# Dilated attention: input laid out by residues, and projections with the weights stationary

## The chip, the cores and the metric

The kernel runs on one core of a Trainium2 chip. The metric is the device time of one execution in microseconds (us); less is better. The core's engines are TensorE (PE, with its weight loads listed apart as PEld), VectorE (DVE), ScalarE (ACT), GpSimd (POOL) and SyncE (SP, which issues most of the transfers). [...]

## The reference

Two transformer blocks, one after the other, on 512 tokens of width 1024. The change lies in the first half of the second block, dilated attention:

```python
DILATED_PATTERNS = ((128, 1), (512, 4), (2048, 16))     # window, dilation
proj = (x @ w_in).reshape(B, S, 3 groups, 3 (q, k, v), 16 heads, 64)
for g, (window, dilation) in enumerate(DILATED_PATTERNS):
    q = rotary(proj[:, :, g, 0], pos)
    k = rotary(proj[:, :, g, 1], pos)
    o, lse = dilated_window_attention(q, k, proj[:, :, g, 2], window, dilation)
...
wts = softmax(stack(lses)); o = sum(wts * outs); return o @ w_out
```

In a group with dilation d a query sees itself and the 128 tokens before it that have the same residue modulo d (as far as they exist). `rotary` turns each head's two halves of 32 features against each other by an angle that depends on the token: `x1*cos - x2*sin` and `x2*cos + x1*sin`.

## The kernel before

Products in full precision are made of three matmuls (`mm3`, lines 161 to 163): every operand is kept as a high part and a low part, and high x high, high x low and low x high are summed in PSUM. Weights arrive by DMA in chunks of 1 MB (1024 rows, 256 columns), two buffers deep; ACT makes the high part (line 187) and DVE, now and then POOL, the low part (line 188), again two buffers deep.

The input of dilated attention, `xT`, is feature-major: tiles with features on the partitions and the 512 tokens as columns in their order. `turn` (line 417) fills it from the residual, one tile of 128 tokens at a time: transposes on PE (line 422), then the split into high (ACT, line 247) and low (DVE, line 248). Each is put off under a key until a step needs it.

`dilated` (line 1386) works in four rounds of four heads, that is two pairs of heads. In a round `project` makes nine chunks, queries, keys and values (s = 0, 1, 2) of three groups g, each with 256 columns of weights. A chunk is four steps, one for each tile of 128 tokens: `project_one` holds the tokens of `xT` stationary and moves 256 columns of weights past them, 8 feature blocks x 3 matmuls = 24 per step, 96 per chunk. For the values of the second and third group a step takes not a tile of neighbouring tokens but the tokens of one residue modulo 4: every fourth column of `xT` (`kx` with step 4).

The result of a step is token-major. Queries and keys are rotated there by DVE (four operations, lines 1436, 1438 and 1440), then turned to feature-major, as the scores want them: two transposes (line 1445), put off by two steps, and two copies by ACT (lines 1451 and 1457), which also sort the tokens by residue, except for the keys of the first group. Values stay token-major and are copied by ACT (lines 1425 and 1428).

33 steps of the first round run alone. After that the loop over rounds works through 16 units per round (a head and a block of 128 queries). `unit` emits, in this order: the scores of a unit (lines 1494 and 1501) with masked maximum, exponential and sum (lines 1482 to 1485); some projection steps of the next round (`fill(0)`); the transposes of the unit before it (`flip`, lines 1510 and 1512), with their copies out of PSUM by ACT (line 1514) and DVE (line 1515); more steps (`fill(1)`); the value products of that unit (lines 1526 and 1529). The fourth round's units are interleaved with the output projection instead. The order on each engine is fixed when the kernel is built, by a scheduler that follows the order of the code but can put an instruction whose operands are free earlier ahead of those that wait. Eight PSUM banks serve all of it.

Of the kernel before, what the change touches and what calls it, by code (L numbers as in the profile page):

```python
# [28 lines left out]
# ---------------------------------------------------------------- constants of the shapes  # L29
# [15 lines left out]
def constants():  # L45
# [11 lines left out]
    rot = np.concatenate([_tok_tiles(np.concatenate([c, c], 1)), _tok_tiles(np.concatenate([-s, s], 1))], 1)  # L57
# [22 lines left out]
    c4, i = rows // 32, rows % 32  # L80
    for j in range(4):
        t = 128 * j + 4 * i + c4
        first = 0 if j == 0 else 128 * (j - 1)
        keys = np.arange(first, 128 * (j + 1))
# [26 lines left out]
class Net:  # L111
# [14 lines left out]
    # ------------------------------------------------------------ small helpers  # L126
# [41 lines left out]
    def wchunk(self, segs, kt, n):  # L168
        """Weights [kt*128, n] gathered from column segments (part slice, k slice, column, source)."""
# [44 lines left out]
    def need(self, *keys):  # L214
        """Emits all that was put off up to the last of keys (all of it without keys)."""
# [3 lines left out]
    def only(self, key):  # L219
        """Emits what was put off under one key, ahead of the rest."""  # L220
# [15 lines left out]
    def rsqrt_act(self, st, scale, eps):  # L236
        """The same where the tables of ScalarE are not in use for exponentials."""
# [3 lines left out]
    def split_to(self, hi, lo, src):  # L241
        """src (SBUF, full precision) into its two parts."""
# [7 lines left out]
    # ------------------------------------------------------------ setup  # L250
    def setup(self):
# [34 lines left out]
        # the parts of a modulation's row stand two partitions apart  # L286
# [17 lines left out]
    def load_cols(self, names, eng):  # L304
        """Vectors of features as columns, turned from rows."""
# [39 lines left out]
    def mod_rows(self, ps, raw, more=False):  # L345
        """Four partial sums of the two rows of a modulation, 32 partitions apart."""
# [5 lines left out]
    def row_parts(self, out, ps):  # L352
        """Rows of a modulation, their high parts on partitions r of 32 and the low ones on r + 2."""
# [4 lines left out]
    def mod_unit(self, i, u):  # L358
        """Columns u*256.. of layer i's modulation: rows for a gate, else turned to per-feature columns."""
# [32 lines left out]
    def affine(self, i, which):  # L392
        """Per-feature factor and shift of the modulated norm, [128, 8, 2 (latent, context)]."""
# [21 lines left out]
    # ------------------------------------------------------------ norm and turn  # L415
    def turn(self, n, xh, xl, c0, a=None, b=None, every=2):
# [27 lines left out]
    def kx(x, k, c0, n, step=1):  # L444
        """k-th 128 features of pair tiles x = (hi, lo), columns c0.."""
        if step == 1:
            return x[0][k // 2][:, k % 2, c0:c0 + n], x[1][k // 2][:, k % 2, c0:c0 + n]
        return x[0][k // 2][:, k % 2, c0:c0 + (n - 1) * step + 1:step], x[1][k // 2][:, k % 2, c0:c0 + (n - 1) * step + 1:step]

    def ssq(self, x, hf, ss):  # L450
        """Sum of squares of half hf of x into ss[:, hf]."""
# [16 lines left out]
    # ------------------------------------------------------------ squared-relu MLP  # L468
    def mlp(self, width, xT, w1, w2, ranges, tiles, sink, lag=3):
# [16 lines left out]
        def chunk():  # L486
            """The next 256 hidden features: weights, and tiles of their parts."""
# [36 lines left out]
    def skew(tiles, lag):  # L524
        """(0, tile) and (1, tile) over the tiles, the second following the first by lag tiles."""
# [6 lines left out]
    # ============================================================ first block  # L532
# [3 lines left out]
    def gains(self, i):  # L536
        """Head gains on every partition."""
# [3 lines left out]
        n = 0  # L541
# [8 lines left out]
    def tables(self, at, eng):  # L550
        """Rope tables with the head gains folded in."""
# [23 lines left out]
    def rope(self, dst, ps, nh, tab, tt, tmp):  # L575
        """dst = gains and (for latent tokens, over the last rw columns) rotation of nh heads."""
# [16 lines left out]
    def heads(self, ps, nh, w, tab, tt, out, sq, t1, t2):  # L593
        """Normed, gained, rotated heads of ps [128, nh*w] into out [128, nh, w]."""
# [9 lines left out]
    # ------------------------------------------------------------ attention over all tokens  # L604
    def attention(self, i, jobs):
        """jobs: dicts of prep (emits what the job needs, returns (kind, q, k, v)), mix tile, fill steps."""
# [4 lines left out]
        def ring(tag, n, width, size):  # L611
            """Space n of a ring of size in the tiles of weights, which are taken as they are needed."""
# [68 lines left out]
        def emit(v, u):  # L681
            """Scores of unit v between the turns and products of unit u."""
# [35 lines left out]
    def mix_parts(self, j, m):  # L718
        """Half m of a pair of mixed features that was kept whole, into its parts."""
# [21 lines left out]
    def first(self, cols):  # L741
        """First layer: its input and the first projection, a quarter of the features at a time as their modulation
        comes in. Returns the input tiles and the projection's sums."""
# [47 lines left out]
        def units(s):  # L791
            """Rows of the modulation of quarter s."""
# [8 lines left out]
        def columns(s):  # L801
            """The modulation's columns of quarter s."""
# [19 lines left out]
        def features(s, tp):  # L822
            """The parts of the features of quarter s of a pair of token tiles."""
# [59 lines left out]
    def layer(self, i, xT, tab, sums=None):  # L883
# [32 lines left out]
        # ckv | kr | cq (first half)  # L916
# [20 lines left out]
        # cq (second half) | q heads 0 3  # L937
# [21 lines left out]
        # k heads | v heads  # L959
# [6 lines left out]
        # q heads 1 4 2 5  # L966
# [5 lines left out]
        def stacked(src, toks, hi, lo=None):  # L972
            """Pairs of heads turned into parts over both halves of the rows: hi with lo, or (hi, lo) each twice."""
# [16 lines left out]
        # pool input; meanwhile the keys of the heads that share them  # L990
# [28 lines left out]
        # second projections of the latent-rank heads, a pair of heads at a time  # L1019
# [97 lines left out]
        # output projection, gated into the residual  # L1117
# [8 lines left out]
        def weights(c):  # L1126
            """A quarter of the output projection's columns, rows as the mixed features lie."""
# [111 lines left out]
    # ============================================================ second block  # L1239
# [5 lines left out]
    def ln_rows(self, name, i):  # L1245
        """Gain and shift of a layer norm on every partition."""
# [13 lines left out]
    def ln_turn(self, j, name, i, rows, xT, wait=2, table=True):  # L1260
        """Layer norm of token tile j: to feature-major parts, and in place as the next residual."""
# [19 lines left out]
        def finish():  # L1281
            """The last norm of token tile j, out to memory."""
# [102 lines left out]
    # ------------------------------------------------------------ dilated attention  # L1385
    def dilated(self, xT):
# [6 lines left out]
        nc.sync.dma_start(m1[:, 512:1024], t["k_rot"])  # L1393
        rot = m1[:, 512:1024].rearrange("p (a t c) -> p a t c", a=2, t=4)
        masks = [m0[:, 0:192], m0[:, 192:576], m0[:, 576:1024], m1[:, 0:512]]

        def project(r, order):
            """Steps that project, rotate and turn the four heads of round r, two pairs; the tiles they fill."""
# [12 lines left out]
            def project_one(g, s):  # L1411
                c0 = (g * 3 + s) * 1024 + r * 256
                wc = self.wcols(w, [(c0, c0 + 256)])
                place(g, s)
                for j in range(4):
# [6 lines left out]
                    if s == 2:  # L1422
                        pv = ps.rearrange("p (a c) -> p a c", a=2)
                        if g == 2:
                            nc.scalar.activation(T["w"][:, :, j, :], pv, AF.Copy)
                        else:
# [461 lines left out]
```

## Time and profile before

| | before |
|---|---|
| median of 3 runs | 3301.78 us (3300.62 to 3303.79) |
| span of the profiled execution | 3301.2 us |
| time around that span | not listed by the profile |
| PE busy | 3238.5 us, 98% |
| PE weight loads | 2807.8 us, 85% |
| DVE busy | 1776.6 us, 54% |
| ACT busy | 1265.7 us, 38% |
| POOL busy | 376.2 us, 11% |
| moved by DMA | 281.62 MB, mean 85 GB/s |
| projections of dilated attention | about 1622 to 2240 us of the span |

All times come from one execution taken by the hardware profiler. Matmuls overlap: one starts while the one before it still drains, so PE's busy time says that PE was never empty, not how fast it went. How fast a stream goes is read from the distances between the starts of its matmuls.

### The profile page before, as it was taken

The page shows a single profiled execution, that of the slowest core. Times are in us where ns is not written, and L with a number is a line of the kernel's source. Part 1 is how long each engine was busy: PE and PEld are TensorE (multiplying, and loading weights), DVE is VectorE, ACT ScalarE, POOL GpSimd, SP SyncE. Part 2 cuts the span into 40 slices and gives each one's busy share as a digit, 9 for nine tenths or more (in the row PEclk, how much of TensorE's full clock was granted, in tenths as well). Part 3 has the DMA queues.
Part 4 walks back from the last instruction along what each step waited for, and adds up shares of the span by engine and source line. Part 5 has one row for each costly group of instructions (what it writes and reads, how often), then busy time and mean ns, then how long its engine had stood idle before and what let it go on. Part 6 is the DMA issues. An engine that isn't in the chain of part 4 may idle for free.

```text
span 3301.2 us, 52357 instructions
## 1 busy us (share of the span) xinstructions
PE 3238.5 (98%) x21704; PEld 2807.8 (85%) x21704; DVE 1776.6 (54%) x3550; ACT 1265.7 (38%) x2549; POOL 376.2 (11%) x541
## 2 busy tenths in 40 slices
PE   7999999999999999999999999999999999989998
PEld 6877988788889788888899999998888878888887
DVE  6677554444466866555644343435544467664445
ACT  4566432222236754222223333334322246542222
POOL 4343100000004420000000000001100030030000
PEclk9999999999999999999999999999999999999999
DMA  7132233333321022322321112112223222133332
GB/s 215 51 103 91 77 104 113 105 115 115 115 58 49 1 66 89 102 90 91 102 77 65 55 62 65 52 55 71 94 90 102 98 73 65 64 103 102 94 98 77
DMA packets 246509, 281.62 MB, mean 85 GB/s; under 512 B 19518, under 2 KB 208384, under 8 KB 246272
## 3 DMA queue, kind: packets, MB, share of 16 engines
q1 hardware_dynamic: 244528, 273.28, 26.0%
q10 hardware_dynamic: 1584, 4.98, 0.4%
q8 instruction: 171, 2.80, 0.4%
q14 instruction: 66, 0.54, 0.1%
q0 software_dynamic: 160, 0.02, 0.0%
HBM read 276.16 MB, written 2.10 MB: 84 GB/s over the span
## 4 chain that ended last, share of the span: by engine, by line
PE 80%; issue 11%; DVE 4%; ACT 2%; POOL 1%; DMA 1%; SPq 0%; ACTq 0%; DVEq 0%; POOLq 0%
PE b L161 18%; PE b L162 18%; PE b L163 18%; PE s L161 4%; PE s L163 4%; PE s L162 4%; PE b L671 2%; PE b L655 2%; PE b L349 1%; PE s L633 1%; DVE t L248 1%; DVE wl L188 1%; PE b L1529 1%; PE b L1445 1%; PE b L1526 1%
## 5 line engine op out<-in xcount | busy, mean ns | idle before, releaser
L161 PE MATMUL b<-wh,t 128*128 128x256 f32 (+2 forms) x2948 | 986.6, 335 | 1.5 <-ACT t L247 1.0
L162 PE MATMUL b<-wl,t 128*128 128x256 f32 (+2 forms) x2948 | 968.3, 328 | 3.9 <-DVE wl L188 3.9
L163 PE MATMUL b<-wh,t 128*128 128x256 f32 (+2 forms) x2948 | 968.8, 329 | 2.7 <-DVE t L248 2.7
L187 ACT ACTIVATE wh<-wr 128x2048 fp32r<-128x2048 f32 (+4 forms) x253 | 389.2, 1549 | 895.1 <-PE b L163 547.3
L188 DVE TENSOR_TENSOR wl<-wr,wh 128x2048 fp32r<-128x2048 f32 (+4 forms) x237 | 460.5, 1947 | 416.6 <-ACT wh L187 415.7
L161 PEld LDWEIGHTS b<-wh,t 128*128 128x128 f32 x2948 | 595.2, 202 | 53.8 <-issue 4.5
L162 PEld LDWEIGHTS b<-wl,t 128*128 128x128 f32 x2948 | 596.5, 202 | 44.3 <-DVE wl L188 4.5
L163 PEld LDWEIGHTS b<-wh,t 128*128 128x128 f32 x2948 | 595.9, 202 | 44.3 <-DVE t L248 3.5
L161 PE MATMUL b<-t,wh 128*128 128x512 f32 (+1 forms) x1232 | 440.8, 359 | 3.0 <-ACT t L247 3.0
L162 PE MATMUL b<-t,wh 128*128 128x512 f32 (+1 forms) x1232 | 439.4, 357 | 1.1 <-DVE t L248 1.1
L163 PE MATMUL b<-t,wl 128*128 128x512 f32 (+1 forms) x1232 | 439.1, 357 | 1.0 <-DVE wl L188 1.0
L161 PEld LDWEIGHTS b<-t,wh 128*128 128x128 f32 x1232 | 233.4, 190 | 39.7 <-ACT t L247 3.4
L163 PEld LDWEIGHTS b<-t,wl 128*128 128x128 f32 x1232 | 233.7, 190 | 35.6 <-DVE wl L188 1.4
L162 PEld LDWEIGHTS b<-t,wh 128*128 128x128 f32 x1232 | 233.7, 190 | 35.2 <-DVE t L248 1.6
L243 DVE CAST t<-h 128x512 fp32r<-128x512 f32 (+1 forms) x176 | 66.1, 377 | 241.2 <-ACT h L481 241.0
L480 ACT ACTIVATE h<-b 128x512 f32<-128x512 f32 (+1 forms) x138 | 70.8, 513 | 220.6 <-PE b L163 220.6
L1186 DVE TENSOR_TENSOR h<-b,gate 128x512 f32<-128x512 f32 (+1 forms) x141 | 89.0, 631 | 120.0 <-PE b L163 119.9
L161 PE MATMUL s<-wh,t 128*128 128x256 f32 (+2 forms) x428 | 146.8, 343 | 1.7 <-ACT h L927 1.0
L1321 DVE TENSOR_TENSOR xl<-xl,b 128x512 f32<-128x512 f32 x128 | 87.3, 683 | 111.3 <-PE b L163 111.3
L162 PE MATMUL s<-wl,t 128*128 128x256 f32 (+2 forms) x428 | 144.1, 337 | 0.0
L163 PE MATMUL s<-wh,t 128*128 128x256 f32 (+2 forms) x428 | 144.1, 337 | 0.0
L647 POOL TENSOR_SCALAR wl<-wl,st 128x768 f32<-128x768 f32 (+1 forms) x120 | 103.6, 864 | 160.6 <-DVE st L646 132.8
(363 smaller groups left out, 4515.5 us busy)
## 6 DMA issues: line engine op xcount, KB each, us to landing
wr<-in_w_mlp SPq DMA_DIRECT2D x64, 1024.0 KB, 5.3
wr<-in_w_mod SPq DMA_DIRECT2D x44, 1024.0 KB, 5.3
wr<-in_attn_w_in SPq DMA_DIRECT2D x36, 1024.0 KB, 5.0
wr<-in_ffn_w_up SPq DMA_DIRECT2D x32, 1024.0 KB, 5.4
wr<-in_ffn_w_down SPq DMA_DIRECT2D x32, 1024.0 KB, 5.0
wr<-in_hgrn_w_in SPq DMA_DIRECT2D x12, 1024.0 KB, 5.1
wr<-in_w_out SPq DMA_DIRECT2D x8, 640.0 KB, 5.1
wr<-in_w_in SPq DMA_DIRECT2D x4, 1024.0 KB
```

Of the source, the lines that this page charges most:

```text
L161: mm(out, a[0], b[0], start=start, stop=False)
L162: mm(out, a[0], b[1], start=False, stop=False)
L163: mm(out, a[1], b[0], start=False, stop=stop)
L187: nc.scalar.activation(hv, rv[:, k], AF.Copy)
L188: (self.aid if cut > 1 and m % 2 else nc.vector).tensor_sub(lv, rv[:, k], hv.bitcast(F32))
L243: self.nc.vector.tensor_copy(hi, src)
L480: nc.scalar.activation(r, ps, AF.Relu)
L647: nc.gpsimd.tensor_scalar(P[:, :n], P[:, :n], sm, 1.0, op0=ALU.mult, op1=ALU.mult)
L655: nc.tensor.transpose(ps[:, kk, a * 128:(a + 1) * 128], u["P"][e, a][:, k0:k0 + 128], self.ident)
L671: nc.tensor.matmul(u["O"][64 * e:64 * e + 64, :256], v[:, k, e * 64:(e + 1) * 64], u["PT"][e, k2][:, kk, :], start=(k == 0), stop=(k == u[ ...
L1186: nc.vector.tensor_mul(tmp, ps, g[:, c0:c0 + n])
L1321: self.nc.vector.tensor_add(x, x, ps)
```

## The change

The columns of `xT` in dilated attention now lie by residue of the token modulo 4: first the 128 tokens with residue 0, then 1, 2, 3. `turn` writes them so, in four runs of 32 for each token tile.

Queries and keys of all groups and the values of the first group are projected the other way round: 128 columns of weights are stationary and all 512 tokens move. A chunk has two halves, one for each pair of heads, of 8 x 3 = 24 matmuls each, and the result is feature-major already, in one PSUM bank. A half is two steps (after feature block 3 and at its end), so a chunk is still four steps. The very first chunk of the first round moves 256 tokens at a time, in four runs of 64, for which two token tiles must be there.

The rotation is done in that layout: ACT copies the four blocks of 32 partitions crosswise out of PSUM, DVE multiplies the product by a cosine table, the crosswise copy by a sine table, and adds. The tables are made feature-major by the host constants, twice as large as before (the second one is a tile and a load of its own). No transposes of queries and keys are left. The first group's values come feature-major and are copied by ACT, turned by four transposes for each pair of heads, put off by two steps, and copied again.

The values of the second and third group keep tokens stationary; a residue is now 128 neighbouring columns of `xT`. The keys of the first group and their masks follow the new order inside each tile.

```diff
     def turn(...):
...
             for pr in range(2):
-                hi, lo = xh[2 * hf + pr][:, :, c0:c0 + 128], xl[2 * hf + pr][:, :, c0:c0 + 128]
-                self.split_psum(hi, lo, h[:, 2 * pr:2 * pr + 2, :])
+                src = h[:, 2 * pr:2 * pr + 2, :]
+                if residues:
+                    i0 = c0 // 4
+                    hi, lo = (x[2 * hf + pr].rearrange("p k (c i) -> p k c i", c=4)[:, :, :, i0:i0 + 32] for x in (xh, xl))
+                    src = src.rearrange("p k (i c) -> p k c i", c=4)
+                else:
+                    hi, lo = xh[2 * hf + pr][:, :, c0:c0 + 128], xl[2 * hf + pr][:, :, c0:c0 + 128]
+                self.split_psum(hi, lo, src)
...
-        nc.sync.dma_start(m1[:, 512:1024], t["k_rot"])
-        rot = m1[:, 512:1024].rearrange("p (a t c) -> p a t c", a=2, t=4)
+        cos, sin = m1[:, 512:1024], self.b2.tile([128, 512], F32, tag="sin", name="sin")
+        nc.sync.dma_start(cos, t["k_rot"][:, 0:512])
+        nc.sync.dma_start(sin, t["k_rot"][:, 512:1024])
...
+            by_tile = lambda x: x.rearrange("p (j c i) -> p c j i", j=4, c=4)
+            by_res = lambda x: x.rearrange("p (c j i) -> p c j i", j=4, c=4)
+
+            def rotate(ps, dst, g, sc):
+                sw, t1 = self.half(), self.half()
+                for q in range(4):
+                    o = q ^ 1
+                    nc.scalar.activation(sw[32 * q:32 * q + 32], ps[32 * o:32 * o + 32], AF.Copy, scale=sc)
+                nc.vector.scalar_tensor_tensor(t1, ps, sc, cos, op0=ALU.mult, op1=ALU.mult)
+                nc.vector.tensor_mul(sw, sw, sin)
+                if g == 0:
+                    nc.vector.tensor_add(by_tile(dst), by_res(t1), by_res(sw))
+                else:
+                    nc.vector.tensor_add(dst, t1, sw)
+
+            def by_feature(g, s, wc, a, ps):
+                if s < 2:
+                    rotate(ps, T[g, a][:, s, :], g, 0.125 if s == 0 else 1.0)
+                    return
+                v = self.half()
+                nc.scalar.activation(by_tile(v), by_res(ps), AF.Copy)
+
+                def turn():
+                    pt = self.bank()
+                    for j in range(4):
+                        nc.tensor.transpose(pt[:, j * 128:(j + 1) * 128], v[:, j * 128:(j + 1) * 128], self.ident)
+                    nc.scalar.activation(T["v"][a][:, 0], pt.rearrange("p (j c) -> p j c", j=4), AF.Copy)
+
+                self.later(2, turn, ("turn", r))
+
-            def project_one(g, s):
+            def project_one(g, s, first=False):
...
+                if first:
+                    ps = [self.bank(), self.bank()]
+                    for tp in range(2):
+                        self.need(("h", 256 * tp), ("h", 256 * tp + 128))
+                        for a in range(2):
+                            out = ps[a].rearrange("p (c t) -> p c t", c=4)[:, :, 64 * tp:64 * tp + 64]
+                            for k in range(8):
+                                self.mm3(out, wk(k, a), self.kr(xT, k, 256 * tp), k == 0, k == 7)
+                            self.tick()
+                            if tp:
+                                by_feature(g, s, wc, a, ps[a])
+                            yield
+                    return
+                if s < 2 or g == 0:
+                    for a in range(2):
+                        ps = self.bank()
+                        for k in range(8):
+                            self.mm3(ps, wk(k, a), self.kx(xT, k, 0, 512), k == 0, k == 7)
+                            if k == 3:
+                                self.tick()
+                                yield
+                        self.tick()
+                        by_feature(g, s, wc, a, ps)
+                        yield
+                    return
                 for j in range(4):
-                    self.need(*[("h", c) for c in ((0, 128, 256, 384) if s == 2 and g else (j * 128,))])
                     ps = self.bank()[:, :256]
                     for k in range(8):
-                        x = self.kx(xT, k, j, 128, 4) if s == 2 and g else self.kx(xT, k, j * 128, 128)
-                        self.mm3(ps, x, (wc[0][:, k, :], wc[1][:, k, :]), k == 0, k == 7)
+                        self.mm3(ps, self.kx(xT, k, j * 128, 128), (wc[0][:, k, :], wc[1][:, k, :]), k == 0, k == 7)
...
```

What the diff takes out besides is the token-major rotation and `turn` of queries and keys, which the functions above show.

## Rows read from the trace of the kernel before

**Rows 1.** The page's busy line: busy us of each engine, share, instructions.
```profile
PE 3238.5 (98%) x21704; PEld 2807.8 (85%) x21704; DVE 1776.6 (54%) x3550; ACT 1265.7 (38%) x2549; POOL 376.2 (11%) x541
```
**Rows 2.** Windows, first overlapped round: length, busy us (instructions) per engine, clock, DMA.
```profile
1740.00:1906.00 166.00, 166.00 (x1621) 160.00 (x1619) 68.22 (x193) 54.47 (x153) 0.00 (x0) 1.00 0.20 64
```
**Rows 3.** Timeline of PE, strided values: start us, us, engine, line, operation, shapes, count.
```profile
1686.64 0.48 PE L161 MATMUL b<-wh,t 128*128 128x256 f32 x1
1686.96 0.40 PE L162 MATMUL b<-wl,t 128*128 128x256 f32 x1
...
1692.10 0.40 PE L163 MATMUL b<-wh,t 128*128 128x256 f32 x1
```
**Rows 4.** Timeline of PE, a step whose stationary columns are neighbours.
```profile
1801.07 0.28 PE L161 MATMUL b<-wh,t 128*128 128x256 f32 x1
...
1803.34 0.28 PE L162 MATMUL b<-wl,t 128*128 128x256 f32 x1
```
**Rows 5.** Timeline of PE's weight loads, last before and second after the values begin.
```profile
1686.27 0.19 PEld L163 LDWEIGHTS b<-wh,t 128*128 128x128 f32 x1
...
1687.06 0.33 PEld L163 LDWEIGHTS b<-wh,t 128*128 128x128 f32 x1
```
**Rows 6.** Lines of PEld in 1622:1740 and 1740:2240: count, busy us, mean ns.
```profile
L163 PEld LDWEIGHTS b<-wh,t 128*128 128x128 f32 x264 | 56.0, 212 | 2.0 <-DVE t L248 2.0
...
L162 PEld LDWEIGHTS b<-wl,t 128*128 128x128 f32 x888 | 199.9, 225 | 0.0
```
**Rows 7.** Timeline of PE, 512 columns moving: FFN stream, and after small matmuls.
```profile
2500.03 0.39 PE L162 MATMUL b<-wl,t 128*128 128x512 f32 x1
...
2507.96 0.39 PE L161 MATMUL b<-wh,t 128*128 128x512 f32 x1
...
2842.10 0.40 PE L163 MATMUL b<-t,wl 128*128 128x512 f32 x1
...
2843.49 0.39 PE L163 MATMUL b<-t,wl 128*128 128x512 f32 x1
```
**Rows 8.** Timeline of PE around one pair of transposes.
```profile
1680.20 0.28 PE L163 MATMUL b<-wh,t 128*128 128x256 f32 x1
1680.32 0.38 PE L1445 MATMUL b<-ident,h 128*128 128x128 f32 x2
...
1680.78 0.28 PE L163 MATMUL b<-wh,t 128*128 128x256 f32 x1
```
**Rows 9.** Lines of ACT by form, whole span: copies out of PSUM.
```profile
L480 ACT ACTIVATE h<-b 128x512 f32<-128x512 f32 x88 | 51.8, 589 | 168.6 <-PE b L163 168.6
L1457 ACT ACTIVATE t<-b 128x128 f32<-128x128 f32 x160 | 35.0, 274 | 84.1 <-PE b L1445 84.1
```
**Rows 10.** Timeline of ACT: the high part of a chunk of weights.
```profile
1674.03 1.92 ACT L187 ACTIVATE wh<-wr 128x2048 fp32r<-128x2048 f32 x1 [2.43 <-PE b L163]
```
**Rows 11.** Lines of DVE by form, 1740:2240.
```profile
L188 DVE TENSOR_TENSOR wl<-wr,wh 128x2048 fp32r<-128x2048 f32 x26 | 59.6, 2292 | 44.5 <-ACT wh L187 44.1
L1438 DVE TENSOR_TENSOR h<-b,t 128x128 f32<-128x128 f32 x144 | 34.4, 280 | 0.0
L1436 DVE TENSOR_TENSOR h<-b,t 128x256 f32<-128x256 f32 x72 | 30.4, 422 | 79.6 <-PE b L163 79.6
...
L1482 DVE CUSTOM_DVE_ANT_0 h<-b,t 128x512 f32<-128x512 f32 x12 | 8.2, 685 | 5.2 <-PE b L1501 5.2
...
L1515 DVE COPY pt<-b 64x256 f32<-64x256 f32 x12 | 4.9, 409 | 0.0
```
**Rows 12.** Lines of ACT by form, 1740:2240: the copy of turned probabilities.
```profile
L1514 ACT ACTIVATE pt<-b 128x256 f32<-128x256 f32 x36 | 13.9, 386 | 3.7 <-PE b L1512 3.0
```
**Rows 13.** Timeline of PE where dilated attention begins; in brackets idle time and releaser.
```profile
1618.96 1.09 PE L422 MATMUL b<-ident,xl 128*128 128x128 f32 x8 [0.79 <-DVE h L1186]
1620.72 0.39 PE L161 MATMUL b<-wh,t 128*128 128x256 f32 x1 [0.67 <-ACT t L247]
...
1623.32 0.39 PE L163 MATMUL b<-wh,t 128*128 128x256 f32 x1 [1.77 <-DVE t L248]
```

More of the change, by code (lines that the diff above doesn't have):

```diff
@@ L56, in constants @@
     c, s = np.cos(ang).astype(np.float32), np.sin(ang).astype(np.float32)
[L57 removed]
+    by_res = lambda a: np.concatenate([a, a], 1).T.reshape(128, 128, 4).transpose(0, 2, 1).reshape(128, 512)
+    rot = np.ascontiguousarray(np.concatenate([by_res(np.concatenate([c, c], 1)), by_res(np.concatenate([-s, s], 1))], 1))
     band = np.zeros((128, 4, 400), np.float32)
@@ L80, in constants @@
     c4, i = rows // 32, rows % 32
+    order = (128 * np.arange(4)[:, None] + (4 * i + c4)[None, :]).reshape(-1)
     for j in range(4):
@@ L83, in constants @@
         first = 0 if j == 0 else 128 * (j - 1)
-        keys = np.arange(first, 128 * (j + 1))
+        keys = order[first:128 * (j + 1)]
         d = t[:, None] - keys[None, :]
@@ L413, in gate, with turn @@
         return o
-    def turn(self, n, xh, xl, c0, a=None, b=None, every=2):
+    def turn(self, n, xh, xl, c0, a=None, b=None, every=2, residues=False):
         nc = self.nc
@@ L443, in kx, with kr @@
     @staticmethod
[L444 to L448, printed above, removed]
+    def kx(x, k, c0, n):
+        return x[0][k // 2][:, k % 2, c0:c0 + n], x[1][k // 2][:, k % 2, c0:c0 + n]
+    @staticmethod
+    def kr(x, k, t0):
+        i0 = t0 // 4
+        return [y[k // 2][:, k % 2, :].rearrange("p (c i) -> p c i", c=4)[:, :, i0:i0 + 64] for y in x]
     def ssq(self, x, hf, ss):
@@ L1421, in project_one @@
                     self.tick()
[L1422 to L1426, printed above, removed]
-                            for a in range(2):
-                                nc.scalar.activation(T["v"][a][:, g, j, :], pv[:, a], AF.Copy)
-                        yield
-                        continue
-                    p3 = ps.rearrange("p (h c) -> p h c", h=4)
@@ L1432, in project_one @@
-                    W = self.half()
-                    t1 = W[:, 0:256].rearrange("p (h c) -> p h c", h=4)
-                    t2 = W[:, 256:512].rearrange("p (h c) -> p h c", h=4)
-                    o = W[:, 0:256]
-                    nc.vector.tensor_mul(t1, p3, rot[:, 0, j:j + 1, :].to_broadcast([128, 4, 64]))
-                    for h in range(2):
-                        nc.vector.tensor_mul(t2[:, :, 32 * h:32 * h + 32], p3[:, :, 32 * (1 - h):32 * (2 - h)],
-                                             rot[:, 1, j:j + 1, 32 * h:32 * h + 32].to_broadcast([128, 4, 32]))
@@ L1440, in project_one @@
-                    nc.vector.tensor_add(o, W[:, 0:256], W[:, 256:512])
-                    def turn(j=j, o=o):
-                        pt = self.bank()[:, :256].rearrange("p (a c) -> p a c", a=2)
-                        for a in range(2):
-                            nc.tensor.transpose(pt[:, a, :], o[:, a * 128:(a + 1) * 128], self.ident)
-                        sc = 0.125 if s == 0 else 1.0
-                        pv = pt.rearrange("p a (i c) -> p a c i", c=4)
-                        for a in range(2):
-                            dst = T[g, a][:, s, :]
-                            if g == 0 and s == 1:
-                                nc.scalar.activation(dst[:, j * 128:(j + 1) * 128], pt[:, a], AF.Copy, scale=sc)
-                                continue
-                            if g == 0:
-                                ov = dst[:, j * 128:(j + 1) * 128].rearrange("p (c i) -> p c i", c=4)
-                            else:
-                                ov = dst.rearrange("p (c i) -> p c i", c=4)[:, :, 32 * j:32 * j + 32]
-                            nc.scalar.activation(ov, pv[:, a], AF.Copy, scale=sc)
@@ L1459, in project_one @@
-                    self.later(2, turn, ("turn", r))
+                    pv = ps.rearrange("p (a c) -> p a c", a=2)
+                    if g == 2:
+                        nc.scalar.activation(T["w"][:, :, j, :], pv, AF.Copy)
+                    else:
+                        for a in range(2):
+                            nc.scalar.activation(T["v"][a][:, g, j, :], pv[:, a], AF.Copy)
                     yield
             def steps():
-                for g, s in order:
-                    yield from project_one(g, s)
+                for n, (g, s) in enumerate(order):
+                    yield from project_one(g, s, r == 0 and n == 0)
@@ L1837, in block2 @@
             for j in range(4):
-                self.later(99, lambda j=j: self.turn([self.xl[:, j, :512], self.xl[:, j, 512:]], xT[0], xT[1], j * 128),
+                self.later(99, lambda j=j: self.turn([self.xl[:, j, :512], self.xl[:, j, 512:]], xT[0], xT[1], j * 128,
+                                                     residues=True),
                            ("h", j * 128))
```

1 line of the change is left out of this document (added).

## The prediction

> **What bounds the kernel now.** I read the page's busy line first: PE is busy for 98% of the span, every other engine for at most 54% [rows 1] (PEld is PE's own weight loading). Such a share is not a proof, so I went to the stretch that the change touches, by windows. Dilated attention begins near 1622 us and its projections end near 2240 us; in the three rounds that overlap projections with attention PE shows no idle time at all, while ACT is busy for a third and DVE for 41% (the first of three windows alike) [rows 2]. So what this stage costs is the sum of PE's instructions, and a change is worth what it takes off PE's issue times, unless it makes PE wait. A matmul's busy time is no measure of that (matmuls overlap); the distance from one start to the next is. I took these distances from the timeline, for each form of matmul that the change removes or adds.
>
> **The strided values.** The code makes values of the second and third group with every fourth token as stationary columns: 4 rounds x 2 chunks x 96 = 768 matmuls. From 1686.96 to 1692.10 us there are 22 distances in 5.14 us, 0.2336 us each [rows 3]; the same form (256 columns moving, same tiles) with neighbouring columns goes at 2.27 us / 19 = 0.1195 us [rows 4]. The weight loads say why: 0.33 us where the stride is 4, 0.19 us where it is 1 [rows 5]. That this holds for all 768 follows from the mean load in the two windows, 212 and 225 ns [rows 6], near 0.221, the mean of 0.33 for 768 and 0.19 for 2688 loads. After the change the input lies by residues, so these stationary columns are neighbours: 768 x (0.2336 - 0.1195) = 87.6 us less on PE. Bounds: nothing (if the stride is not what makes these loads slow) and 87.6; I take 87.6, because the forms differ in nothing else.
>
> [...] The trace has 330 ns against 190 ns for equal counts, so I go by the trace.
>
> **512 columns moving.** 28 chunks (queries and keys of all groups, first values, four rounds) had 96 matmuls of 256 columns; 27 of them now have 48 of 512 (the first chunk stays at 256, in runs of 64, so that it can start on half the tokens). Two of the old cost 0.2390 us. One of the new, in this kernel's FFN, goes at 0.2266 us in a long stream (2500.03 to 2507.96, 35 distances), but at 0.2317 us just after a run of small matmuls (2842.10 to 2843.49, 6 distances) [rows 7]. In the 6 chunks ahead of the rounds I use the first: 6 x 48 x 0.0124 = 3.6 us. In the rounds each step of 12 matmuls follows attention's small ones, so the second: 21 x 48 x 0.0073 = 7.4 us. Together 11.0 us; bounds 0 (0.2390 for the new) and 16 (0.2266 everywhere). [...]
>
> **The turns.** Queries and keys are now made feature-major, so 4 x 6 x 4 = 96 pairs of transposes go. A pair between two projections: L163 at 1680.20 and the L163 two matmuls later at 1680.78, so 0.58 us for what takes 0.36 us without it [rows 8]: 0.22 us a pair, 21.1 us. The first values, now also feature-major, are turned back: 8 x 4 transposes = 16 pairs, 3.5 us added.
>
> **The other engines, off the path if nothing queues.** Per chunk of queries or keys ACT loses 8 copies of 0.27 us (2.2 us) and gets 8 of 32 x 512 from PSUM. No row has that shape; nearest is 128 x 512 from PSUM, 0.589 us, and below it the 128 x 128 copy's 0.274 us [rows 9]. I take 0.59, the one with as many columns: 4.7 us, with the weights' high part (1.92 us [rows 10]) 6.6 us under a chunk of 48 x 0.23 = 11 us of PE. DVE loses 4 x (0.42 + 2 x 0.28 + 0.42) = 5.6 us (the sum of cosine and sine parts is as wide as the cosine product) and gets 2 x 3 operations of 128 x 512 at about 0.69 us (the masked maximum's 0.685 us is the nearest row) [rows 11], 4.1 us, less than before. Price on PE: nothing from the sums. The strided reads and writes of the residues' layout are the same kind that ACT did before in its turned copies, at the same 0.274 us.
>
> What is not free is order. ACT's four swaps of a half chunk start when its last matmul ends and take 4 x 0.59 = 2.4 us; then DVE multiplies and adds, 1.4 us. The copies of the turned probabilities (0.39 us on ACT, 0.41 us on DVE [rows 11, 12]), for which the value matmuls wait, can queue behind them and end 4.2 us after that matmul. PE's cover is the four transposes (0.44 us) and one step of 12 matmuls (2.8 us): 3.2 us, so 1.0 us short. In three rounds are 48 units; in about 19 of them (every second step, 7 of 9 chunks) the end of a half chunk falls there: up to 19 us. Before, 2.29 us of DVE's weight splitting could fall in the same place and PE still showed no idle time, so the schedule often puts copies ahead. I take 8 us; bounds 0 and 28 (1.5 us each).
>
> **The start.** Before, the first projection needed one token tile: PE started at 1620.72 us and waited again for DVE's parts until 1623.32 [rows 13]. Now the first half needs two tiles: 8 more transposes (1.1 us) and 4 more splits on DVE (128 x 256 from PSUM, as the 0.42 us row of the cosine product: 1.7 us) before it runs freely. I take 3 us; bounds 0 and 6. The second rotation table adds one 256 KB load on SP's queue, a few tenths of a us at an issue about 0.4 us long, behind which a weights' transfer waits; it is needed only when the first rotation begins, and costs nothing unless the weights come last.
>
> **Sum.** 87.6 + 11.0 + 21.1 - 3.5 = 116.2 us off PE, less 8 and 3: 105 us. The profiled execution's span is 3301.2 us (what lies around it is not shown), 0.6 us under the median 3301.78: 3301.8 - 105 = 3197 us.
>
> **Rivals.**
> - *The stalls are real (18%).* ACT's bursts put 1.5 us into all 19 units and the new matmuls go at the upper bound: 116 - 11 - 28 - 6 = 71 us gained, 3231 us; halfway to it 3215. For: ACT goes from a third to over half busy in the rounds. Against: half busy, and a unit's chain has one unit of slack in every other place.
> - *The stride was not the reason (4%).* If the 768 matmuls keep 0.2336 us, 105 - 88 = 17 us remain: 3285 us. The mechanism would be something else in these chunks that stays, such as their place in the order. Against it: the loads' 0.33 us beside 0.19 us in the chunk just before, of the same tiles. [...]
> - *Slower (3%).* The next chunk's split (1.92 us ACT, then 2.29 us DVE) falls in ACT's queue behind the last half's four swaps, which wait for the chunk's last matmul: PE then stands 2.4 + 1.9 + 2.3 = 6.6 us at each of 35 chunk ends, 231 us, so 3301.8 - 116 + 231 = 3417 us. It turns the sign from 18 chunks on. Against: now the split starts a whole chunk ahead (at 1674.03 us for weights first used at 1686.64) [rows 10, 3], because two buffers of weights allow it, and that stays.
> - *It moves nothing (1%).* The edit leaves PE's stream as it is, and the time stays at 3302: the code rules it out, short of a wait that exactly eats the gain.
>
> **Numbers.** The forecast with its own terms (3180 to 3212) has 74%. Its low end has no stalls, 0.2266 throughout and no loss at the start: 116 + 5 (16 in place of 11) gives 3301.8 - 121 = 3181; the stall rival reaches 3231. The low end of the range goes 5 us under that, for switches between small and projection matmuls, of which I counted none as saved. The range 3176 to 3226 leaves out the far half of the stall rival and the three last: below 20%. A difference of 0.2% (6.6 us) is about what a measurement of this kernel can tell from none. Faster by more: 95%; within: 2%; slower by more: 3%.
>
> **What would show it.** Right: loads of 0.19 us for all values' chunks; a round (166 us before) near 135 us; 512-column matmuls 0.227 to 0.232 us apart in the stage; no pairs of turns of queries and keys; PE idle under 15 us between 1622 us and the stage's end. Wrong: idle time on PE ahead of the value products released by the probabilities' copies (the first rival), or ahead of a chunk's first matmul released by the split (the slower one); the values' loads still at 0.33 us.

## The result and the profile after

The changed kernel takes 3184.68 us (median of 4 runs, 3183.46 to 3188.13); the kernel before, run beside it, 3302.78 us (3300.62 to 3305.57). The ratio is 0.9644 [0.963, 0.9658], a gain of 118.1 us where 105 was forecast. The profiled execution has a span of 3185.9 us and was itself the longest of the four, 3188.13 us. One execution of a kernel below (every crosswise copy twice) took 3824.61 us at a granted clock of 0.752 and is left out of its comparison.

The page's busy line after answers to [rows 1]. The share of PE has not moved; the same 98% belongs to a shorter span. There are 1456 matmuls fewer (1296 by the wider ones, 160 by the turns); the strided ones are as many as before, and faster.

```profile
PE 3123.6 (98%) x20248; PEld 2634.5 (83%) x20248; DVE 1754.7 (55%) x3310; ACT 1344.0 (42%) x2533; POOL 376.3 (12%) x541
```

To find where it went, I cut both spans at the start of the first block's last matmul and at the first and the last scores of dilated attention (matmuls of line 1494 before, of 1533 after), us:

| stretch | before | after | gain |
|---|---|---|---|
| up to the end of the first block | 1617.8 | 1620.3 | -2.5 |
| from there to the first scores | 122.3 | 101.6 | 20.7 |
| first to last scores | 557.7 | 460.8 | 96.9 |
| the rest | 1003.5 | 1003.3 | 0.2 |

The code ahead, which the change does not touch, was 2.5 us slower in this one execution. All the rest of the difference lies in the two stretches of projections: 117.6 us. These two hardly vary: the changed kernel's second profiled execution, further below, has 101.6 and 460.8 us again (a fall in clock can take some 1.4 us in the first of them, see the end). The last stretch took anything from 999.5 to 1005.0 us over the profiled kernels here. So I compare kernels by the two stretches as well as by their times.

Windows after, as in [rows 2]: 160 us of the rounds, and nearly all that follows the start. PE is never idle, although ACT went from a third to 58% (92.19 of 160).

```profile
1740.00:1900.00 160.00, 160.00 (x1461) 133.26 (x1460) 77.23 (x156) 92.19 (x180) 0.00 (x0) 1.00 0.23 75
...
1640.00:2120.00 480.00, 480.00 (x4099) 405.49 (x4098) 230.41 (x442) 270.56 (x510) 0.00 (x0) 1.00 0.24 76
```

Waits of PE from 1620 to 2183 us (line, what for: us, times, longest). The whole stretch has 3.2 us, and 2.5 of them are at its start (the first two rows).

```profile
PE b L165 <- DVE t L251: 1.7, 1, 1.7
PE b L425 <- DVE h L1199: 0.8, 1, 0.8
PE b L1574 <- ACT o L1570: 0.7, 1, 0.7
```

Timeline of PE in the first chunk of second-group values, which answers to [rows 3]: 52 distances in 6.23 us, 0.1198 us, where they were 0.2336 us.

```profile
1685.59 0.28 PE L164 MATMUL b<-wh,t 128*128 128x256 f32 x1
...
1691.82 0.28 PE L165 MATMUL b<-wl,t 128*128 128x256 f32 x1
```

Lines of PEld after, 1610:2130, for [rows 6]. Both forms, activations stationary and weights stationary, now load in 0.19 us.

```profile
L165 PEld LDWEIGHTS b<-wl,t 128*128 128x128 f32 x272 | 52.0, 191 | 0.4
...
L165 PEld LDWEIGHTS b<-t,wh 128*128 128x128 f32 x464 | 88.2, 190 | 16.6 <-DVE t L251 2.0
```

Timeline of PE, 512 columns moving in the rounds, for [rows 7]: 10 distances in 2.31 us. Over 861 distances of this form in the rounds the mean is 0.2294 us; ahead of them (278) it is 0.2271. Both means leave out the first distance after other matmuls, 0.31 to 0.34 us (72 in the rounds). The 256-column form has a longer one there too, mostly 0.20 or 0.22 us, and by either the switch costs some 0.09 us.

```profile
1742.36 0.40 PE L165 MATMUL b<-t,wh 128*128 128x512 f32 x1
...
1744.67 0.39 PE L166 MATMUL b<-t,wl 128*128 128x512 f32 x1
```

Lines of ACT and of DVE after, 1610:2240: the crosswise copy and the cosine product, the shapes for which [rows 9, 11] gave only neighbours.

```profile
L1433 ACT ACTIVATE h<-b 32x512 f32<-32x512 f32 x192 | 113.3, 590 | 27.8 <-PE b L166 25.2
```
```profile
L1434 DVE SCALAR_TENSOR_TENSOR h<-b,t 128x512 f32<-128x512 f32 x48 | 33.2, 692 | 72.5 <-ACT h L1433 67.7 <-PE b L1568 2.3
```

### The profile page after: what moved, and what is told of

The parts are those of the page before. It is cut to its first block, busy times and chain, and to the rows that moved or that the text cites. A ratio compares the mean times of both kernels' runs of the same rounds, so it can differ in the third digit from the quotient of the medians.

```text
span 3185.9 us, 49101 instructions
## 1 busy us (share of the span) xinstructions
PE 3123.6 (98%) x20248; PEld 2634.5 (83%) x20248; DVE 1754.7 (55%) x3310; ACT 1344.0 (42%) x2533; POOL 376.3 (12%) x541
## 4 chain that ended last, share of the span: by engine, by line
PE 80%; issue 11%; DVE 4%; ACT 2%; POOL 1%; DMA 0%; SPq 0%; ACTq 0%; DVEq 0%; POOLq 0%
PE b L164 18%; PE b L166 17%; PE b L165 17%; PE s L164 5%; PE s L166 4%; PE s L165 4%; PE b L684 2%; PE b L668 2%; PE b L352 2%; PE s L646 1%; DVE t L251 1%; DVE wl L191 1%; PE b L1568 1%; PE b L1565 1%; PE b L1533 1%
## 5 line engine op out<-in xcount | busy, mean ns | idle before, releaser
L164 PE MATMUL b<-wh,t 128*128 128x256 f32 (+2 forms) x2052 | 694.9, 339 | 0.4 <-ACT h L940 0.2
L165 PE MATMUL b<-wl,t 128*128 128x256 f32 (+2 forms) x2052 | 686.2, 334 | 3.9 <-DVE wl L191 3.9
L166 PE MATMUL b<-wh,t 128*128 128x256 f32 (+2 forms) x2052 | 686.1, 335 | 1.5 <-DVE t L251 1.5
L164 PE MATMUL b<-t,wh 128*128 128x512 f32 (+1 forms) x1696 | 626.2, 370 | 3.1 <-ACT t L250 3.0
L165 PE MATMUL b<-t,wh 128*128 128x512 f32 (+1 forms) x1696 | 616.9, 364 | 2.8 <-DVE t L251 2.8
L166 PE MATMUL b<-t,wl 128*128 128x512 f32 (+1 forms) x1696 | 617.3, 364 | 1.0 <-DVE wl L191 1.0
L164 PEld LDWEIGHTS b<-wh,t 128*128 128x128 f32 x2052 | 389.0, 190 | 48.0 <-issue 3.5
L165 PEld LDWEIGHTS b<-wl,t 128*128 128x128 f32 x2052 | 389.4, 190 | 44.5 <-DVE wl L191 4.5
L166 PEld LDWEIGHTS b<-wh,t 128*128 128x128 f32 x2052 | 389.2, 190 | 43.1 <-DVE t L251 2.3
L164 PEld LDWEIGHTS b<-t,wh 128*128 128x128 f32 x1696 | 320.6, 190 | 59.1 <-ACT t L250 4.0
L166 PEld LDWEIGHTS b<-t,wl 128*128 128x128 f32 x1696 | 320.7, 189 | 53.7 <-DVE wl L191 1.4
L165 PEld LDWEIGHTS b<-t,wh 128*128 128x128 f32 x1696 | 321.3, 189 | 52.0 <-DVE t L251 3.6
L1433 ACT ACTIVATE h<-b 32x512 f32<-32x512 f32 x192 | 113.3, 590 | 27.8 <-PE b L166 25.2
```

The lines of the kernel that those rows point to most:

```text
L164: mm(out, a[0], b[0], start=start, stop=False)
L165: mm(out, a[0], b[1], start=False, stop=False)
L166: mm(out, a[1], b[0], start=False, stop=stop)
L1433: nc.scalar.activation(sw[32 * q:32 * q + 32], ps[32 * o:32 * o + 32], AF.Copy, scale=sc)
```

## The experiments

**The layout put back.** Theory: stationary columns four apart cost 0.114 us a matmul, and that alone is three quarters of the gain. Rival: the loads were slow for some other reason. The changed kernel, with its second- and third-group values' stationary columns four apart again (other tokens than the result needs, the same amount of work):

```diff
-    self.mm3(ps, self.kx(xT, k, j * 128, 128), ...)
+    x = [y[k // 2][:, k % 2, j:j + 509:4] for y in xT]
+    self.mm3(ps, x, ...)
```

> The changed kernel, but the values of the second and third group take every fourth column of xT as stationary operand again (in the new layout these are other tokens, so these values are wrong; nothing else differs). Theory (the stride of the stationary columns costs the time): 768 x (0.2336 - 0.1195) = 87.6 us more than the changed kernel, 3272 us, loads of 0.33 us. Rival (something else in these chunks cost it, the stride did not): 3185 us, loads of 0.19 us.

Measured: 3271.92 us (3269.71 to 3273.97), ratio to before 0.9903 [0.9889, 0.9916]; 87.2 us more than the changed kernel. The two stretches of projections are 75.0 and 11.9 us longer, 86.9 in all. The timeline of PE has the old distance back (29 of them in 6.77 us, 0.2334 us), and that of PEld the old load:

```profile
1683.61 0.39 PE L166 MATMUL b<-wh,t 128*128 128x256 f32 x1
...
1690.38 0.39 PE L165 MATMUL b<-wl,t 128*128 128x256 f32 x1
```
```profile
1683.71 0.33 PEld L164 LDWEIGHTS b<-wh,t 128*128 128x128 f32 x1
```

**Neighbouring columns in the kernel before.** The same question from the other side (again other tokens):

```diff
-    x = self.kx(xT, k, j, 128, 4) if s == 2 and g else self.kx(xT, k, j * 128, 128)
+    x = self.kx(xT, k, j * 128, 128)
```

> The kernel before, but the values of the second and third group take 128 neighbouring columns of xT (the tokens of a tile instead of those of a residue, so these values are wrong). Theory: 87.6 us less than before, 3215 us, loads of 0.19 us in all chunks. Rival (the gain needs the weights held stationary): 3303 us. With the changed kernel at 3185, what is left between 3215 and 3185, 30 us, is the work of the weights-stationary part by itself (11 us of matmuls, 17.6 us of turns and what the forecast took off for waits).

Measured: 3216.85 us (3213.22 to 3219.63), ratio 0.9736 [0.9722, 0.9749], 87.2 us less than the kernel before (3304.06 beside it); the two stretches are 74.6 and 12.3 us shorter, some 87 in all. The mean load is 192 ns:

```profile
L162 PEld LDWEIGHTS b<-wl,t 128*128 128x128 f32 x1256 | 241.0, 192 | 0.4
```

The stride is worth the same in both kernels, within 1 us by the stretches, so it neither hides nor adds to the other edits. (That the times agree to a tenth is luck: those of one kernel spread by 4 to 6 us.) What is left between this kernel and the changed one, 3216.85 - 3184.68 = 32.2 us, is what turning the projections round is worth; the stretches say 30.7.

**Two and three columns apart.** Is it the stride of four or any stride? Second group two apart, third group three apart:

```diff
-    self.mm3(ps, self.kx(xT, k, j * 128, 128), ...)
+    x = [y[k // 2][:, k % 2, j:j + 127 * (g + 1) + 1:g + 1] for y in xT]
+    self.mm3(ps, x, ...)
```

> The changed kernel with stationary columns 2 apart (8 bytes) for the second group's values and 3 apart (12 bytes) for the third group's; these values are of other tokens. If any stride costs: both chunks at 0.2336 us a matmul, 3272 us. If only a stride of 16 bytes costs: both at 0.12 us, 3185 us. [...]

Measured: 3212.02 us (one run). In PE's timeline, two apart costs nothing (0.117 us, 3 distances) and three apart goes at 0.173 us ahead of the rounds (6 distances in 1.04 us) and at 0.177 over the whole stage (355 distances); PEld's timeline has 0.26 us for that load:

```profile
1685.61 0.28 PE L164 MATMUL b<-wh,t 128*128 128x256 f32 x1
...
1685.96 0.28 PE L164 MATMUL b<-wh,t 128*128 128x256 f32 x1
...
1721.81 0.34 PE L166 MATMUL b<-wh,t 128*128 128x256 f32 x1
...
1722.85 0.34 PE L166 MATMUL b<-wh,t 128*128 128x256 f32 x1
```
```profile
1722.03 0.26 PEld L165 LDWEIGHTS b<-wl,t 128*128 128x128 f32 x1
```

By the stage's mean 384 matmuls three apart should cost 384 x (0.177 - 0.120) = 21.9 us. The two stretches of projections are 22.5 us longer than in the changed kernel; the spans differ by 23.9 and the single time by 27.3, and those last us are not accounted for. So neither is it any stride that costs, nor four alone: per matmul two apart adds nothing, three apart 0.057 us, and four apart 0.114 us, twice that. What makes the loads of three and four slow, and what other strides cost, is not shown by these runs.

**512 as two times 256.** Theory: two matmuls of 256 columns cost some 0.012 us more than one of 512 (forecast 11 us in all). Against it stands the forecast's lower bound, that they cost no more. The changed kernel, the weights still stationary:

```diff
-    for k in range(8):
-        self.mm3(ps, wk(k, a), self.kx(xT, k, 0, 512), k == 0, k == 7)
-        ...
+    for m in range(2):
+        for k in range(8):
+            self.mm3(ps[:, 256 * m:256 * m + 256], wk(k, a), self.kx(xT, k, 256 * m, 256), k == 0, k == 7)
+        ...
```

> The changed kernel, but every matmul with 512 tokens moving is made as two of 256 with the same weights loaded twice (27 chunks, 1296 matmuls more; same results). Theory (distance of two at 256 is 0.2390 us, of one at 512 in the changed kernel 0.2271 ahead of the rounds and 0.2294 in them): 6 x 48 x 0.0119 + 21 x 48 x 0.0096 = 13 us more, 3198 us; the forecast had 11. [...]

Measured: 3199.5 us (3195.15 to 3201.67), ratio 0.968 [0.9667, 0.9693]: 14.8 us more than the changed kernel (the spans differ by 13.5). First to last scores took 470.4 us, 9.6 more; from the distances it should be 21 x 48 x (0.2390 - 0.2294) = 9.7. With 3.6 us ahead of them it is 13.3 in the two stretches. The bound of nothing falls. Of the 32.2 us above, 17.4 are left for the turns and whatever the start lost; by the stretches, 30.7 - 13.3 = 17.4 too.

**Every crosswise copy twice.** Theory: there is room for ACT's bursts, so twice the bursts costs at most a few us. Rival: they are at the edge of stalling PE, and doubling them brings the stalls in.

```diff
+    for _ in range(2):
         nc.scalar.activation(sw[32 * q:32 * q + 32], ps[32 * o:32 * o + 32], AF.Copy, scale=sc)
```

> The changed kernel with each of ACT's crosswise copies made twice (192 more copies of 32 x 512, 0.59 us each, 113 us of ACT; same results). Theory (the order fixed at build time puts the copies that PE waits for ahead, and ACT at half load has room): no more than 5 us, 3185 to 3190 us, PE without idle time in the rounds. Rival (the forecast's first rival: bursts of ACT stand ahead of the probabilities' copies): a burst is now 4.8 us, against 3.2 us of cover; 2.4 us in each of 19 units and more, 3230 us or above.

Measured: 3187.04, 3187.06 and 3192.49 us, ratio 0.9651 [0.9637, 0.9666]; 2.4 us more by the median of the three, and 4.2 us more in the two stretches of the trace. ACT is busy for 79% of the window below, and PE still stands for only 3.1 us in 484. The second fence is the largest of PE's waits there: it is for the exponentials, not for the copies of turned probabilities.

```profile
1640.00:2124.00 484.00, 480.94 (x4096) 404.93 (x4095) 225.87 (x442) 383.78 (x702) 0.00 (x0) 1.00 0.23 75
```
```profile
PE b L1550 <- ACT h L1524: 2.6, 4, 1.3
```

**The start with all four token tiles.** Theory: the first chunk's special form, 256 tokens at a time, saves a wait. Rival: other work fills it anyway. Here the first chunk waits for all tokens:

```diff
-    for tp in range(2):
-        self.need(("h", 256 * tp), ("h", 256 * tp + 128))
-        ... (256 tokens at a time)
+    self.need(*[("h", 128 * j) for j in range(4)])
```

> The changed kernel without the first chunk's halves of 256 tokens: it waits for all four token tiles and then moves 512 like the rest (same results). Theory (PE waits for the turned input at the start): 16 more transposes (2 us) and 8 more splits on DVE (3.4 us) ahead of the first free-running matmul, 0.6 us back from wider matmuls, and more matmuls at the lower clock: 3 to 7 us more, 3188 to 3191 us. Rival (the start is hidden or bound by something else): 3184 to 3185 us.

Measured: 3183.82 us (3183.31 to 3187.58), ratio 0.9639 [0.9625, 0.9652]: no measurable difference, as the rival had it; the theory said 3 to 7 us more. From the first transposes of the stage to the first scores it is 1.1 us longer: PE's waits at the start come to 4.6 us instead of 2.5, and the wider matmuls of the first chunk give part of that back. The special form of the first chunk is worth 1.1 us.

**The start without GpSimd's splits.** What PE waits for there is DVE, as the chain of waits of the changed kernel says (start us, us, what):

```profile
1620.72 0.64 ACT wh L190
1621.38 0.69 DVE wl L191
1622.08 1.71 DVE xl L1200
1623.78 1.68 DVE wl L191
1625.46 0.68 DVE t L251 x2
1626.18 0.39 PE b L165
```

GpSimd's two splits stand in its timeline from 1621.95:

```profile
1621.95 2.96 POOL L191 TENSOR_TENSOR wl<-wr,wh 128x512 fp32r<-128x512 f32 x2 [8.20 <-ACT wh L190]
```

Beside them two of DVE's operations hold the chain for 1.7 us each; the one just before them, of the same 128 x 512 shape, holds it for 0.69 us. So DVE makes these parts itself in dilated attention:

```diff
-    self.cut = 2
+    self.cut, self.aid = 2, self.nc.vector
...
+    self.aid = nc.gpsimd     # at the end of dilated attention
```

> The changed kernel, but the first two chunks of weights of dilated attention are split into low parts by DVE alone and not by DVE and POOL in turn (same results). In the changed kernel a 128 x 512 split takes DVE 1.75 us while POOL runs, 0.69 us alone, and the first low parts of xT start at 1625.38 us behind them. Theory (DVE and POOL slow each other, which holds up the start, and PE's granted clock falls in the wait): DVE is free at about 1623, 2 to 4 us gained, 3181 us, and 1620 to 1632 at full clock. Rival (DVE's two pieces more, 1.4 us, eat it): 3184 to 3186 us.

Measured: 3183.54 us (3182.32 to 3185.82), ratio 0.9635 [0.9622, 0.9648]. Windows of the changed kernel's start, and then of this one (us busy of PE, PEld, DVE, ACT and POOL, then the granted clock):

```profile
1620.00:1626.00 6.00, 3.59 (x25) 2.63 (x24) 5.28 (x6) 2.91 (x7) 2.96 (x2) 1.00 0.56 192
1626.00:1632.00 6.00, 5.82 (x35) 5.82 (x36) 3.02 (x9) 2.36 (x8) 0.00 (x0) 0.72 0.60 201
```
```profile
1620.00:1626.00 6.00, 5.93 (x50) 5.63 (x49) 5.98 (x15) 4.41 (x14) 0.00 (x0) 1.00 0.86 290
1626.00:1632.00 6.00, 5.96 (x49) 5.63 (x48) 2.19 (x6) 1.70 (x5) 0.00 (x0) 1.00 0.32 106
```

PE's wait for DVE's parts is gone (0.8 us ahead of the first transposes stay), DVE's operations take 0.69 us again, and the lower clock is gone too. From the first transposes to the first scores it takes 97.0 us instead of 100.4: 1.7 us are the wait, and about 1.4 the matmuls at the lower clock (15 of them 0.213 us apart instead of 0.12). But the whole time moves by less than the spread of the runs. So all of it once more on one chip, with a third kernel that takes GpSimd out of the splits of the whole second block:

```diff
-    self.ps, self.bs, self.aid = None, {}, nc.gpsimd
+    self.ps, self.bs, self.aid = None, {}, nc.vector
```

The changed kernel again:

> The changed kernel itself, on the same chip as the two below, as their yardstick: 3185 us by its first runs.

Without GpSimd in dilated attention, again:

> The changed kernel with DVE alone splitting the first two chunks of dilated attention. Its trace showed the stretch from the first block's last matmul to the first scores at 98.2 us, against 101.6 us in the changed kernel's. Theory (that stretch is on the path and nothing after gives it back): 3.4 us less than the changed kernel beside it. Rival (the difference was that of two profiled executions, the clock falls in some and not in others): less than 1 us.

Without it in the whole block:

> As the kernel above, and the first two chunks of both FFNs and of the gated recurrence too are split by DVE alone. Theory (POOL's help slows DVE where DVE already has the norm's work): 1 to 5 us less than with dilated attention alone. Rival (there POOL is busy with the norm's gains, DVE has no time, two pieces more on DVE delay the parts of the input): the same or up to 4 us more.

Measured: 3186.4 (3183.98 to 3187.03), 3184.15 (3180.04 to 3185.13) and 3183.1 us (3178.21 to 3184.96); ratios 0.9645 [0.9632, 0.9658], 0.9637 [0.9624, 0.9651] and 0.9634 [0.9621, 0.9647]. In the stage, 100.4, 97.0 and 97.0 us again. That the start is 3.4 us shorter is shown three times, against two executions of the changed kernel in which the clock fell; that the whole kernel is 2 to 3 us faster is likely, but the intervals overlap, and it stays open.

## Why the prediction was right, and where it was off

The mechanism was right: the stage was the sum of PE's distances, and the gain is what came off them. With the sizes measured after (0.22 us a pair of turns is still the forecast's):

- *Between first and last scores:* 648 strided matmuls at 0.114, 73.9; 512 columns 9.7; 72 pairs of turns less 12, 13.2. Sum 96.8 us; the traces differ by 96.9, closer than the terms are known (0.01 us a pair is 0.6 us).
- *Ahead of them:* 120 strided matmuls, 13.7; 512 columns 6 x 48 x (0.2390 - 0.2271) = 3.4; 24 pairs less 4, 4.4. Sum 21.5 us; the traces differ by 20.7, which leaves 0.8 us for the start.

**The strided values** (87.6 us forecast) were about 87 us, measured twice in opposite directions. (Ahead of the rounds it gave 11.9 and 12.3 us where 120 x 0.114 = 13.7; as an estimate, the fall of the clock at the start, some 1.4 us in the changed kernel's trace, would make that up if it came in the faster kernel of each pair only, and then it is nearer 88.) The rival that the stride was not the reason falls with it: the same 128 columns loaded in 0.19 us as neighbours, 0.26 three apart and 0.33 four apart.

**512 columns moving** (11.0 us) was under-sized: 13.1 us by the distances, 13.3 by the stretches and 14.8 by the times of the experiment. The slow distance, 0.2317 us, was read from six matmuls just after small ones and put on all 21 chunks of the rounds; the mean over the rounds is 0.2294. The bounds, 0 and 16, held.

**The turns** (17.6 us net) are not measured alone, but are what is left with the start's loss: 17.4 us.

**The stalls** (8 us) are the step that failed. None came: no row of PE's waits between 1640 and 2120 us. The sizes of the bursts were right (0.590 us for each crosswise copy, 0.692 for the products) and the queueing too; what was wrong was the cover. I had read `unit` as making the value products of the unit that it has just turned. It keeps those back by one more unit: `pf, fl = fl, ...flip(...)` takes the turned probabilities of the call before, in both kernels (line 1586 before, 1625 after), and the description of `unit` ahead of the prediction has the same mistake. The first rival's "one unit of slack in every other place" was half of it: every place has it. Timelines of PE, ACT and DVE after, in one such place:

```profile
1744.90 0.38 PE L1549 MATMUL b<-ident,h 128*128 128x128 f32 x2
1745.12 0.38 PE L1551 MATMUL b<-ident,h 128*64 128x128 f32 x2
...
1748.12 0.33 PE L1565 MATMUL b<-t,pt 128*128 128x64 f32 x2
1748.38 0.43 PE L1568 MATMUL b<-t,pt 32*32 32x64 f32 x16
...
1752.72 0.38 PE L1549 MATMUL b<-ident,h 128*128 128x128 f32 x2
...
1758.81 0.56 PE L1565 MATMUL b<-t,pt 128*128 128x64 f32 x4
1759.30 0.43 PE L1568 MATMUL b<-t,pt 64*32 64x64 f32 x16
...
1765.73 0.56 PE L1565 MATMUL b<-t,pt 128*128 128x64 f32 x4
```
```profile
1746.86 2.39 ACT L1433 ACTIVATE h<-b 32x512 f32<-32x512 f32 x4
1749.28 0.39 ACT L1553 ACTIVATE pt<-b 128x256 f32<-128x256 f32 x1
```
```profile
1746.87 2.29 DVE L191 TENSOR_TENSOR wl<-wr,wh 128x2048 fp32r<-128x2048 f32 x1 [2.04 <-ACT wh L190]
1749.29 0.69 DVE L1434 SCALAR_TENSOR_TENSOR h<-b,t 128x512 f32<-128x512 f32 x1
...
1750.49 0.41 DVE L1554 COPY pt<-b 64x256 f32<-64x256 f32 x1
```

A unit is turned at 1744.90, the next at 1752.72, each with 64 keys in its second and third group. ACT's copy of the first does queue behind four crosswise copies, DVE's behind a weight split and a rotation, until 1750.90: 5.6 us after the first unit's transposes (the next matmul starts at 1745.26), longer than the 4.2 I feared. But the products at 1748.12 are those of the unit before it (32 keys wide). Its own start at 1758.81, 7.9 us after that copy and after the next unit has been turned; the next unit's start at 1765.73, 12.7 us after its transposes (1753.07), where the prediction had 3.2. So it is throughout. In the 48 units of the three rounds the copies end up to 5.7 us after the transposes, in 20 of them later than 3.2, and what they take beyond 3.2 us adds up to 28.9 us, about the upper bound of this term. But no unit's products start earlier than 8.5 us after its transposes, nor earlier than 4.5 us after its last copy. That is why twice the crosswise copies cost so little: there the least is still 3.9 us.

**The start** (3 us) was 0.8 us, and that is not the start's own: in the changed kernel's trace PE's clock fell there (0.72 over 1626:1632), which took about 1.4 us, and in the trace of the kernel before it did not (1.00 over the same window). Its reasons were off as well. Two tiles instead of one did not make PE wait longer: its waits there are 2.5 us after (0.8 and 1.7) and were 3.3 us before (0.8, 0.7 and 1.8 [rows 13]), and waiting for all four adds 1.1 us to the stretch. What holds PE is DVE's slow operations beside GpSimd, which stood in the kernel before too: there GpSimd's two splits run from 1619.44 to 1622.38 us, two of DVE's operations beside them take 1.78 and 1.75 us, and the wait until 1623.32 us was of the same kind.

The forecast was 13 us short: 8 for stalls that had a unit of slack, 2 at the start, 2 to 4 for the 512 columns. All three erred the same way, so they did not cancel; the forecast came close because the largest term, three quarters of the gain, was read from the very loads and distances that the change removes.

**The other rivals.** A weight split late behind the crosswise copies would stand in the waits of the chunks' first matmuls; there is none between 1640 and 2120 us. For what was named as evidence: the rounds are 128.7 to 131 us long (start of the first scores to the next), where 135 was written. The 166 us beside it was the length of a window, not of a round; the rounds before took 158 to 160.5 us.

## What to carry to other kernels

Where PE is never idle, price an edit by the distances between starts of the very form that it removes, and read these from a mean over the stage, not from a handful at a switch. Look at the weight loads' own durations: the same count of stationary columns can cost 0.19 or 0.33 us by their stride alone, and a layout that makes them neighbours was worth three quarters of this gain. Before you price a stall, follow in the code which iteration's result the waiting instruction reads; a pipeline one stage deeper than you took it for turns a stall into nothing.

## What the runs showed that I had not expected

- The load of 128 stationary columns takes 0.19 us for neighbours, 0.26 three apart and 0.33 four apart; the matmul stream follows it at 0.12, 0.173 to 0.177 and 0.2336 us, and goes at 0.117 two apart.
- ACT's copy of 32 x 512 out of PSUM takes 0.590 us, as long as 128 x 512 (0.589): fewer partitions bought nothing.
- A DVE operation on 128 x 512 with two operands in SBUF took 0.69 us alone and 1.75 to 1.79 us beside a GpSimd operation of the same kind.
- In the changed kernel's trace the granted clock falls to 0.72 on average over 1626:1632, just after PE's waits at the start of the stage: from 1626.9 to 1630.1, at a granted clock of 0.50, the 256-column matmuls are 0.213 us apart, and then 0.12 again. In its second profiled execution they are 0.213 us apart from 1625.3 to 1628.3 (0.92 over 1620:1626, 0.80 over 1626:1632), and where the first chunk waits for all tokens those of 512 columns are 0.427 us apart from 1628.7 to 1631.3, and then 0.23. The waits do not settle it: the kernel before has 3.3 us of them, and its clock stayed at 1.00. In the three without the 1.7 us wait the 256-column matmuls stayed 0.12 us apart. A trace in which the clock falls is some 1.4 us longer here.
